# Query projections: the order of the weight halves in two of three token tiles, and the PSUM banks and place of the first two score products

## The chip, the cores and the metric

The kernel runs on one core of a Trainium2 chip. The metric is the time of one execution on the device in microseconds (us). Before the change it is 1845.09 us, the median of three runs (1844.77, 1845.09 and 1849.04).

TensorE (PE in the profile) multiplies, VectorE is DVE, ScalarE is ACT, GpSimd is POOL, and SyncE (SP) issues the transfers. Each engine works through its own instructions in the order of the program and waits on semaphores for the others.

## The reference

A diffusion transformer of two layers for 512 latent and 256 context tokens of width 1024: layer 0 mixes by attention with 16 query and 4 key heads of width 64, layer 1 by a gated recurrence, and each is followed by a gated feed-forward part. The change touches the attention of layer 0 alone. What it computes there is, cut to the core:

```python
def queries(h):
    q = (h @ w_q).reshape(b, t, ATTN_KV_HEADS, ATTN_GROUP, HEAD_DIM).transpose(0, 2, 3, 1, 4)
    return rms_norm(q, q_norm)
...
q_l = apply_axial_rope(queries(h_lat), rope)
k_l, v_l = keys_values(h_lat)
...
s = jnp.einsum('bkgqd,bksd->bkgqs', q, k) * (HEAD_DIM ** -0.5)
p = jax.nn.softmax(s, axis=-1)
return jnp.einsum('bkgqs,bksd->bkgqd', p, v)
```

Queries of context tokens are not rotated, and context tokens attend to context keys alone.

## The kernel before

**Products in three parts.** Every fp32 operand is split into a rounded upper part (`whi`, `hnh`) and the rest (`wlo`, `hnl`), and `mm3` (L110) issues three products for one: upper by upper (L112), upper by lower (L113) and lower by upper (L114). The weights of a group are loaded by `load_split` (L93): a transfer into `raw`, ScalarE rounds it into `whi` (L88), VectorE subtracts for `wlo` (L91). There are three buffers each of `whi` and `wlo`.

**Query projections** (L614 to L636). Four groups (g, 0 to 3) of 256 columns, each with two weight halves: half 0 holds the rows k = 0 to 3 of 8, half 1 the rows 4 to 7. In a group there are three tiles (tp, 0 to 2) of 256 tokens, and each tile is one PSUM bank that holds two runs of 128 tokens (tt). A run is 8 k by 3 products, so 24 matmuls of 256 columns, and a tile is 48. The first run takes half 0 and then half 1; the second run takes half 1 and then half 0. Below, "the tile (2,0)" is group 2, tile 0.

**What follows a tile.** `q_first` (L581) calls `qk_norm_rope` (L502), which is a chain over three engines: ACT squares the product (L510), DVE sums (L513) and scales (L514), ACT takes the root (L515), DVE inverts and refines (L516 to L520) and multiplies the product by it (L522, tile `qhat`, the last reader of the bank), DVE multiplies by the cosines (L532) while POOL multiplies by the sines in four pieces (L537), DVE adds both (L541) and rounds (L585), and POOL subtracts (L586). For context tiles (tp 2) one multiplication on POOL (L526) stands in place of L532 to L541. In the very last tile (3,2), L526 and L586 are on DVE. The transposes of a tile (L592, `ptq`, two banks with four transposes each) and their copies on ACT (L595, into `qT`) come three tiles later (`Q_LAG`, L610). The code is in that order; the framework's scheduler then fixes the order of every engine's instructions, and buffers are given out when one is free.

**The passage to the attention** (L648 to L657). The PSUM pool of the projections (four banks for products, three for transposes, one for another sum, `pa`) is closed, and one of two pairs of banks for scores, two banks and two more is opened on the same eight banks. Three tiles are then still to be transposed ((3,0), (3,1), (3,2)); between the first and the second of them the scores of head 0, tile 0 are issued (`score_mm`, L637, four matmuls, tile `sc`). After it, 96 units (16 heads by 6 tiles of 128 tokens) run through `scores` (maximum on DVE L689, exponential on ACT L691), transposes of the probabilities (L703) and products with the values (L714, L715). Beside them TensorE transposes the residual input in eight blocks (`rx`, L671, copied to `hT` by ACT L672) and sums a modulation product (`pa`, L181); `rx` uses the same two pairs of banks as the scores.

Of the kernel before, what the change touches and what calls it, by code (L numbers as in the profile page):

```python
# [18 lines left out]
KT = D // P  # L19
# [28 lines left out]
def kernel(  # L48
# [13 lines left out]
    def pool(name, es=None, **kw):  # L62
        return (es or ctx).enter_context(tc.tile_pool(name=name, bufs=1, reuse_waits="tile", **kw))
# [5 lines left out]
    def psum_pool(**bufs):  # L69
        es = ExitStack()  # L70
        psums["pool"], psums["bufs"] = pool(f"psum{len(bufs)}", es, space=PSUM), bufs
        return es
# [7 lines left out]
    def bank(name):  # L80
        return psums["pool"].tile([P, 512], F32, tag="b", bufs=psums["bufs"]["b"], name=name)
# [28 lines left out]
    def mm3(ps, ahi, alo, bhi, blo, first, last, onto=False):  # L110
        kw = dict(skip_group_check=True) if onto else {}
        PE.matmul(ps, ahi, bhi, start=first, stop=False, **kw)  # L112
        PE.matmul(ps, ahi, blo, start=False, stop=False, **kw)  # L113
        PE.matmul(ps, alo, bhi, start=False, stop=last, **kw)  # L114
# [436 lines left out]
    def k_first(tp):  # L551
        r = qk_norm_rope(kraw[tp].rearrange("p t (h d) -> p t h d", d=HD), tp, "k")
        kd = qst.tile([P, 2, KVH, 2, HD], F32R, tag="sp", bufs=3, name="kd")
        kl = qst.tile([P, 2, KVH, HD], F32R, tag="spl", name="kl")
        for i in range(2):
            DVE.tensor_copy(kd[:, :, :, i].rearrange("p t h d -> p (t h) d"), r.rearrange("p t h d -> p (t h) d"))
        POOL.tensor_tensor(kl, r, kd[:, :, :, 0].bitcast(F32), op=ALU.subtract)

        def second():
            kds = [kd[:, :, g].rearrange("p t a d -> p t (a d)") for g in range(KVH)]  # L560
            kds += [kl[:, :, 2 * i : 2 * i + 2].rearrange("p t a d -> p t (a d)") for i in range(KVH // 2)]
            cs = slice(tp * 256, tp * 256 + 256)
            for i in range(0, len(kds), 2):
                pt = bank("ptk")
                for j in range(2):
                    for tt in range(2):
                        PE.transpose(pt[:, (2 * j + tt) * P : (2 * j + tt + 1) * P],
                                     kds[i + j][:, tt].bitcast(F32), ident)
                pg = pt.rearrange("p (g t) -> p g t", g=2)
                if i < KVH:  # L570
                    ACT.copy(kTt[:, i : i + 2, cs], pg)
                    continue
                for j in range(2):
                    dst = kTt[:, KVH + j : 2 * KVH : 2, cs]
                    rows = slice(j * HD, (j + 1) * HD)
                    ACT.copy(dst[0:HD], pg[rows])
                    DVE.tensor_copy(dst[HD:P], pg[rows])

        return second
# [18 lines left out]

    pes.close()
    pes = psum_pool(q=4, b=3, a=1)  # L600
    apsum = psums["pool"].tile([P, 512], F32, tag="a", name="pa")

    def qbank(name):
        return psums["pool"].tile([P, 512], F32, tag="q", bufs=psums["bufs"]["q"], name=name)
# [3 lines left out]
    later = []  # L608
# [7 lines left out]
    for g in range(KVH):  # L616
        ws = []
        for i in range(2):
            src = attn_w_qkv[0, 512 * i : 512 * (i + 1), g * 256 : (g + 1) * 256].rearrange("(k p) n -> p k n", p=P)
            ws.append(load_split(src, [P, 4, 256], f"wq{g}{i}"))  # L620
        for tp in range(3):
            psf = qbank(f"q{g}{tp}")
            for tt in range(2):
                ts_ = slice((tp * 2 + tt) * P, (tp * 2 + tt + 1) * P)
                ks = list(range(KT)) if tt == 0 else list(range(4, KT)) + list(range(4))
                for k in ks:
                    wh, wl = ws[k // 4]
                    mm3(psf[:, tt * 256 : tt * 256 + 256], hn_hi[k][:, ts_], hn_lo[k][:, ts_],
                        wh[:, k % 4], wl[:, k % 4], k == ks[0], k == ks[-1])
            if g == 0:  # L630
                first(k_first, tp)
            first(q_first, g, tp, psf[:, 0:512])
            dfill.step(2)
# [3 lines left out]
    def score_mm(h, t):  # L637
        g, j = h // 4, h % 4
        keys = key_tiles(t)
        nk, k0 = len(keys) * P, keys[0] * P  # L640
        q = qT[g][:, j, t * P : (t + 1) * P]
        ps = s2("sc")
        for a in range(0, nk, 512):
            e = min(nk, a + 512)
            PE.matmul(ps[:, a:e], q, kTh[g][:, k0 + a : k0 + e], start=True, stop=False)  # L645
            PE.matmul(ps[:, a:e], q, kTl[g][:, k0 + a : k0 + e], start=False, stop=True)  # L646
        return ps
# [1 line left out]
    dfill.drain()  # L649
    pes.close()  # L650
    pes = psum_pool(s2=2, b=2, t=2)
    early = {}
    for i, f in enumerate(later):
        f()
        if i == 0:
            early[0, i] = score_mm(0, i)
    qes.close()  # L657

    hpool = pool("hT", side="right")
# [1105 lines left out]
```

## Time and profile before

| what | value |
|---|---|
| median of three runs | 1845.09 us |
| the profiled execution, its time | 1847.34 us |
| the profiled execution, its span from first to last instruction | 1845.5 us |
| PE busy | 1780.8 us (96%) |
| DVE busy | 1224.5 us (66%) |
| ACT busy | 765.9 us (42%) |
| POOL busy | 543.2 us (29%) |
| query projections on PE, start to last product | 76.9 to 173.9 us |

The span is counted from the first instruction of the execution. A row of the timeline names the start, the duration, the engine, the line, the operation, output<-input and the shape; in brackets is the idle time of the engine before it and who ended it. The ends of matmuls are modelled, so the pace of TensorE is read from the starts.

### The profile page before, as it was taken

To read this page: it belongs to the slowest core of one execution; us is meant where nothing else is said; L and a number is where in the kernel's file an instruction comes from. 1 tells how busy PE (TensorE), PEld (TensorE's weight loads), DVE (VectorE), ACT (ScalarE), POOL (GpSimd) and SP (SyncE) were. 2 spreads that over 40 slices of the span, in tenths; PEclk is the share of its full clock that TensorE was granted. 3 is DMA by queue.
4 is the path that set the end of the run, shared out by engine and by line. 5 is a ranking of instruction groups with operands and counts; after the bars stand their busy time and mean duration, and the time that the engine had idled before them with its cause. 6 is when DMAs were issued, how large, how long until landed. Compare 5 with 4: busy or idle time off the path is not lost.

```text
span 1845.5 us, 30295 instructions
## 1 busy us (share of the span) xinstructions
PE 1780.8 (96%) x11929; PEld 1627.0 (88%) x11929; DVE 1224.5 (66%) x2097; ACT 765.9 (42%) x1465; POOL 543.2 (29%) x508
## 2 busy tenths in 40 slices
PE   8979999999999999999999989999998999999998
PEld 6779688988899989898988889898997899898997
DVE  3586688888878787878756475656738774344443
ACT  4333787777533425252545233333323432222234
POOL 1244255445513314141315264443535100000000
PEclk9999999999999999999999999999999999999999
DMA  9433510002033232525231212112211253333321
GB/s 329 160 115 86 166 59 24 14 11 75 23 111 112 71 119 75 154 87 171 63 109 45 69 58 81 59 57 80 80 52 29 86 166 92 93 89 94 100 85 56
DMA packets 213198, 166.41 MB, mean 90 GB/s; under 512 B 7696, under 2 KB 190144, under 8 KB 213056
## 3 DMA queue, kind: packets, MB, share of 16 engines
q1 hardware_dynamic: 212768, 163.43, 28.7%
q8 instruction: 94, 1.54, 0.3%
q10 hardware_dynamic: 288, 1.05, 0.1%
q14 instruction: 48, 0.39, 0.1%
HBM read 162.36 MB, written 2.10 MB: 89 GB/s over the span
## 4 chain that ended last, share of the span: by engine, by line
PE 83%; DVE 8%; ACT 3%; POOL 3%; issue 2%; DMA 1%; POOLq 0%; SPq 0%; DVEq 0%; ACTq 0%
PE ffo L112 5%; PE ffo L113 5%; PE ffo L114 5%; PE ffi L112 5%; PE ffi L113 5%; PE ffi L114 5%; PE pt L703 3%; PE x L112 2%; PE x L113 2%; PE x L114 2%; PE lv L1566 2%; PE hz L112 2%; PE hz L113 2%; PE hz L114 2%; PE sc L645 2%
## 5 line engine op out<-in xcount | busy, mean ns | idle before, releaser
L112 PE MATMUL ffi<-fnh,whi_fi 128*128 128x256 f32 x704 | 198.9, 283 | 0.1
L113 PE MATMUL ffi<-fnl,whi_fi 128*128 128x256 f32 x704 | 198.0, 281 | 0.9 <-DVE fnl L1236 0.9
L114 PE MATMUL ffi<-fnh,wlo_fi 128*128 128x256 f32 x704 | 197.8, 281 | 0.0
L113 PEld LDWEIGHTS ffi<-fnl,whi_fi 128*128 128x128 f32 x704 | 133.2, 189 | 1.5 <-DVE fnl L1236 1.3
L112 PEld LDWEIGHTS ffi<-fnh,whi_fi 128*128 128x128 f32 x704 | 132.7, 189 | 0.5 <-issue 0.3
L114 PEld LDWEIGHTS ffi<-fnh,wlo_fi 128*128 128x128 f32 x704 | 132.8, 189 | 0.0
L676 DVE SCALAR_TENSOR_TENSOR hT<-ffo,modc,hT 128x512 f32<-128x512 f32 (+1 forms) x106 | 67.0, 636 | 90.8 <-PE ffo L114 90.7
L1573 POOL TENSOR_TENSOR KD<-KD,tot 128x384 f32<-128x384 f32 x96 | 101.5, 1081 | 67.8 <-ACT kc L1556 66.2
L280 POOL TENSOR_TENSOR rc<-rc,mhalf 128x2 f32<-128x2 f32 (+2 forms) x7 | 6.3, 906 | 379.3 <-DVE rc L278 379.3
L693 POOL TENSOR_SCALAR pf<-pf,st 128x768 f32<-128x768 f32 (+1 forms) x96 | 73.6, 769 | 127.9 <-DVE st L692 91.6
L88 ACT CAST whi_fi<-raw_fi 128x1024 fp32r<-128x1024 f32 x44 | 46.2, 1051 | 146.7 <-PE ffi L113 72.7
L114 PE MATMUL ffo<-gh,wlo_w 128*128 128x512 f32 (+1 forms) x304 | 102.6, 338 | 0.0
L113 PE MATMUL ffo<-gl,whi_w 128*128 128x512 f32 (+1 forms) x304 | 102.3, 337 | 0.0
L112 PE MATMUL ffo<-gh,whi_w 128*128 128x512 f32 (+1 forms) x304 | 101.6, 337 | 0.0
L91 DVE TENSOR_TENSOR ptl<-pt,pth 128x384 fp32r<-128x384 f32 (+1 forms) x160 | 79.8, 523 | 12.4 <-ACT pth L88 11.2
L1556 ACT COPY kc<-KD 128x256 f32<-128x256 f32 x112 | 43.0, 414 | 102.7 <-PE lv L1566 37.6
L689 DVE TENSOR_REDUCE st<-sc 128x1 f32<-128x768 f32 (+1 forms) x96 | 74.2, 773 | 15.3 <-PE sc L646 12.5
L88 ACT CAST pth<-pt 128x384 fp32r<-128x384 f32 (+1 forms) x160 | 69.9, 461 | 34.2 <-PE pt L703 22.4
L235 DVE SCALAR_TENSOR_TENSOR adacc<-adw,csil,adacc 128x512 f32<-128x512 f32 x98 | 82.0, 850 | 2.1 <-DMA adw<-in_ada_w_dram 1.8
L1573 DVE TENSOR_TENSOR QD<-QD,tot 128x256 f32<-128x256 f32 x96 | 55.5, 619 | 41.1 <-PE lv L1566 40.4
L691 ACT ACTIVATE pf<-sc,st 128x768 f32<-128x768 f32 (+1 forms) x96 | 73.4, 765 | 19.3 <-DVE st L689 18.4
L703 PE MATMUL pt<-ident,pf 128*128 128x128 f32 x448 | 72.2, 276 | 5.1 <-DVE ptl L91 3.9
(852 smaller groups left out, 5980.6 us busy)
## 6 DMA issues: line engine op xcount, KB each, us to landing
raw_fi<-in_ffn_w_in_dram SPq DMA_DIRECT2D x44, 512.0 KB, 3.7
adw<-in_ada_w_dram SPq DMA_DIRECT2D x40, 512.0 KB, 4.5
adw<-in_ada_w_dram SPq DMA_DIRECT2D x80, 256.0 KB, 3.1
raw_hz<-in_hgrn_w_in_dram SPq DMA_DIRECT2D x14, 512.0 KB, 3.6
raw_fo<-in_ffn_w_out_dram SPq DMA_DIRECT2D x16, 448.0 KB, 3.8
adr<-in_ada_w_dram SPq DMA_DIRECT2D x16, 256.0 KB, 4.7
adr<-in_ada_w_dram SPq DMA_DIRECT2D x8, 512.0 KB, 6.8
raw_wq<-in_attn_w_qkv_dram SPq DMA_DIRECT2D x8, 512.0 KB, 6.2
```

The costliest lines, as they stand in the source:

```text
L88: ACT.copy(hi, src)
L91: (eng or DVE).tensor_tensor(lo, src, hi.bitcast(F32), op=ALU.subtract)
L112: PE.matmul(ps, ahi, bhi, start=first, stop=False, **kw)
L113: PE.matmul(ps, ahi, blo, start=False, stop=False, **kw)
L114: PE.matmul(ps, alo, bhi, start=False, stop=last, **kw)
L235: pin(DVE.scalar_tensor_tensor(a, raw, cc, a, op0=ALU.mult, op1=ALU.add))
L676: DVE.scalar_tensor_tensor(hT[o][:, a:e], ps, mcol(layer, ch, o, v), hT[o][:, a:e], op0=ALU.mult, op1=ALU.add)
L689: DVE.tensor_reduce(st3[:, 0:1], ps[:, :nk], op=ALU.max, axis=AX.X, negate=True)
L691: ACT.activation(pf, ps[:, :nk], AF.Exp, bias=st3[:, 0:1], accum_out=st3[:, 1:2])
L693: POOL.tensor_scalar(pf, pf, st3[:, 2:3], 1.0, op0=ALU.mult, op1=ALU.mult)
L703: PE.transpose(pt[:, i * P : (i + 1) * P], pf[:, (i0 + i) * P : (i0 + i + 1) * P], ident)
L1573: eng.tensor_tensor(view, view, f, op=ALU.mult)
```

## The change

Three edits. In the tiles 0 and 2 of each group the four half runs are issued as (run 0, half 0), (run 1, half 0), (run 0, half 1), (run 1, half 1); tile 1 keeps the order of before. Since both runs are then open at once in one bank, the second run's first matmul doesn't carry the start flag. One bank of the transposes is allocated ahead of `pa` and of the products, which turns the banks round. And the scores of the tiles 0 and 1 of head 0 are issued ahead of the transposes of the last three tiles.

```diff
--- before.py
+++ after.py
@@ -561,7 +561,7 @@
             kds += [kl[:, :, 2 * i : 2 * i + 2].rearrange("p t a d -> p t (a d)") for i in range(KVH // 2)]
             cs = slice(tp * 256, tp * 256 + 256)
             for i in range(0, len(kds), 2):
-                pt = bank("ptk")
+                pt = ptk0.pop() if ptk0 else bank("ptk")
                 for j in range(2):
                     for tt in range(2):
                         PE.transpose(pt[:, (2 * j + tt) * P : (2 * j + tt + 1) * P],
@@ -598,6 +598,7 @@
 
     pes.close()
     pes = psum_pool(q=4, b=3, a=1)
+    ptk0 = [bank("ptk")]
     apsum = psums["pool"].tile([P, 512], F32, tag="a", name="pa")
 
     def qbank(name):
@@ -620,13 +621,20 @@
             ws.append(load_split(src, [P, 4, 256], f"wq{g}{i}"))
         for tp in range(3):
             psf = qbank(f"q{g}{tp}")
-            for tt in range(2):
+            half = [range(4), range(4, KT)]
+            if tp == 1:
+                runs = [(0, half[0]), (0, half[1]), (1, half[1]), (1, half[0])]
+            else:
+                runs = [(0, half[0]), (1, half[0]), (0, half[1]), (1, half[1])]
+            seen = [0, 0]
+            for tt, ks in runs:
                 ts_ = slice((tp * 2 + tt) * P, (tp * 2 + tt + 1) * P)
-                ks = list(range(KT)) if tt == 0 else list(range(4, KT)) + list(range(4))
                 for k in ks:
                     wh, wl = ws[k // 4]
+                    seen[tt] += 1
+                    onto = tp != 1 and tt == 1
                     mm3(psf[:, tt * 256 : tt * 256 + 256], hn_hi[k][:, ts_], hn_lo[k][:, ts_],
-                        wh[:, k % 4], wl[:, k % 4], k == ks[0], k == ks[-1])
+                        wh[:, k % 4], wl[:, k % 4], seen[tt] == 1 and not onto, seen[tt] == KT, tp != 1)
             if g == 0:
                 first(k_first, tp)
             first(q_first, g, tp, psf[:, 0:512])
@@ -649,11 +657,9 @@
     dfill.drain()
     pes.close()
     pes = psum_pool(s2=2, b=2, t=2)
-    early = {}
-    for i, f in enumerate(later):
+    early = {(0, t): score_mm(0, t) for t in range(2)}
+    for f in later:
         f()
-        if i == 0:
-            early[0, i] = score_mm(0, i)
     qes.close()
 
     hpool = pool("hT", side="right")
```

On TensorE, in the tile (2,0) from its tenth to its fifteenth matmul, the rows of before are these (`q_1440` is the tile's bank, `whi_wq_1429` and `wlo_wq_1430` are weight half 0 of group 2, `whi_wq_1435` and `wlo_wq_1436` half 1):

```order
L112 MATMUL q_1440<-whi_wq_1429,hnh_90 128x256
L113 MATMUL q_1440<-wlo_wq_1430,hnh_90 128x256
L114 MATMUL q_1440<-whi_wq_1429,hnl_98 128x256
L112 MATMUL q_1440<-whi_wq_1435,hnh_91 128x256
L113 MATMUL q_1440<-wlo_wq_1436,hnh_91 128x256
L114 MATMUL q_1440<-whi_wq_1435,hnl_99 128x256
```

And after it, from the 22nd to the 27th matmul of the same tile:

```order
L112 MATMUL q_1440<-whi_wq_1429,hnh_90 128x256
L113 MATMUL q_1440<-wlo_wq_1430,hnh_90 128x256
L114 MATMUL q_1440<-whi_wq_1429,hnl_98 128x256
L112 MATMUL q_1440<-whi_wq_1435,hnh_91 128x256
L113 MATMUL q_1440<-wlo_wq_1436,hnh_91 128x256
L114 MATMUL q_1440<-whi_wq_1435,hnl_99 128x256
```

The first use of half 1 moved from the 13th to the 25th matmul of the tile. Half 1 of a group takes the buffers of a half of the group before that is last read at the 36th matmul of that group's last tile before, and at the 24th after.

On VectorE one instruction moves, the subtraction for half 1 of group 2. The names are those of the chain of the tile (1,1), whose L532, L541 and L585 these are; L513 and L514 belong to the tile (1,2):

```order
 L532 TENSOR_TENSOR qrot<-qhat,cwq 128x256 x2
+L91 TENSOR_TENSOR wlo_wq_1436<-raw_wq_1434,whi_wq_1435 128x1024
 L541 TENSOR_TENSOR qrot<-qrot,qsin 128x512
 L585 CAST qd<-qrot 128x8x64
-L91 TENSOR_TENSOR wlo_wq_1436<-raw_wq_1434,whi_wq_1435 128x1024
 L513 TENSOR_REDUCE ss<-qrot 128x8
 L514 TENSOR_SCALAR ss<-ss 128x8
```

It stands ahead of the addition now, and behind the rounding before. All other subtractions for query weights keep their places.

On TensorE, behind the last product of the projections, the rows of before are these (`ptq` are transposes of query tiles, `sc` scores, `rx` blocks of the residual input):

```order
L592 MATMUL ptq<-ident,qd 128x128 x16
L645 MATMUL sc<-kT,qT_705 128x512
L646 MATMUL sc<-kT,qT_705 128x512
L645 MATMUL sc<-kT,qT_705 128x256
L646 MATMUL sc<-kT,qT_705 128x256
L592 MATMUL ptq<-ident,qd 128x128 x8
L671 MATMUL rx_2040<-ident,hT_2004 128x128 x2
L592 MATMUL ptq<-ident,qd 128x128 x8
L671 MATMUL rx_2040<-ident,hT_2004 128x128 x4
L181 MATMUL pa<-adw_2120,cpad 32x256 x4
```

And after, where all lines behind the inserted ones have moved by up to eight numbers (L653 is L645 of before):

```order
L592 MATMUL ptq<-ident,qd 128x128 x8
L653 MATMUL sc<-kT,qT_705 128x512
L654 MATMUL sc<-kT,qT_705 128x512
L653 MATMUL sc<-kT,qT_705 128x256
L654 MATMUL sc<-kT,qT_705 128x256
L653 MATMUL sc<-kT,qT_705 128x512
L654 MATMUL sc<-kT,qT_705 128x512
L653 MATMUL sc<-kT,qT_705 128x256
L654 MATMUL sc<-kT,qT_705 128x256
L592 MATMUL ptq<-ident,qd 128x128 x24
L181 MATMUL pa<-adw_2120,cpad 32x256 x4
```

Two scores stand ahead of the 24 transposes of group 3, and no `rx` block stands among them. In the built program the scores' pairs are the banks 0 to 3, which held transposes and `pa` before the passage; the transposes of group 3 alternate between the banks 4 and 5, and bank 5 held the product of the tile (3,2). Before the change, the first scores' pair held the products of (3,1) and (3,2), and the transposes' banks held `pa` and the product of (2,2).

On ScalarE the copy of the first `rx` block stood ahead of the load of the exponential's table and of the first two exponentials; it stands behind them now, so three copies of `rx` blocks stand between the second and the third exponential, and two stood there before. The first `rx` block now takes the bank pair of the first scores and waits for their exponential; the second waits for the second's. From about the 960th of some 10,100 rows of TensorE on, the order of all engines is that of before; that place is at 222 us of the profile.

## Rows read from the trace of the kernel before

**Rows 1.** The page's part on the chain that ended last, shares of the span by engine.

```profile
PE 83%; DVE 8%; ACT 3%; POOL 3%; issue 2%; DMA 1%; POOLq 0%; SPq 0%; DVEq 0%; ACTq 0%
```

**Rows 2.** Who TensorE waited for, longest first: engine, line, releaser, us in total, times, longest. The first two rows are from 60 to 200 us, the third is the only row of the stretch from 182 to 222 us.

```profile
PE q L113 <- DVE wlo_wq L91: 5.1, 1, 5.1
PE sc L645 <- DVE qhat L522: 3.5, 1, 3.5
...
PE pt L703 <- DVE ptl L91: 1.3, 2, 1.1
```

**Rows 3.** The timeline of TensorE in the tile (2,0), and the first matmul of the tile (3,0).

```profile
128.63 0.28 PE L113 MATMUL q<-wlo_wq,hnh 128*128 128x256 f32 x1
...
129.81 0.28 PE L114 MATMUL q<-whi_wq,hnl 128*128 128x256 f32 x1
129.92 0.31 PE L112 MATMUL q<-whi_wq,hnh 128*128 128x256 f32 x1
135.38 0.58 PE L113 MATMUL q<-wlo_wq,hnh 128*128 128x256 f32 x1 [5.15 <-DVE wlo_wq L91]
...
141.05 1.04 PE L592 MATMUL ptq<-ident,qd 128*128 128x128 f32 x8
...
154.81 0.36 PE L112 MATMUL q<-whi_wq,hnh 128*128 128x256 f32 x1
```

**Rows 4.** Stretches: length, busy time of PE, its weight loads, DVE, ACT and POOL (instructions), TensorE's granted clock, DMA share, GB/s.

```profile
135.30:138.50 3.20, 3.12 (x14) 3.12 (x15) 3.03 (x9) 0.21 (x1) 1.18 (x1) 0.50 0.51 165
...
179.20:182.40 3.20, 3.20 (x15) 3.05 (x16) 2.68 (x4) 0.80 (x2) 0.00 (x0) 0.57 1.20 302
```

**Rows 5.** ACT's rounding and DVE's subtraction of weight halves: half 1 of group 2 on ACT, then half 1 of group 3 on ACT and on DVE.

```profile
128.74 1.05 ACT L88 CAST whi_wq<-raw_wq 128x1024 fp32r<-128x1024 f32 x1
...
152.82 1.05 ACT L88 CAST whi_wq<-raw_wq 128x1024 fp32r<-128x1024 f32 x1 [2.83 <-PE q L114]
...
155.31 1.22 DVE L91 TENSOR_TENSOR wlo_wq<-raw_wq,whi_wq 128x1024 fp32r<-128x1024 f32 x1
```

**Rows 6.** The timeline of DVE over the end of the chain of the tile (1,1), all of (1,2) and the start of (2,0). The first L91 is half 1 of group 2, the second half 0 of group 3.

```profile
130.82 1.02 DVE L532 TENSOR_TENSOR qrot<-qhat,cwq 128x256 f32<-128x256 f32 x2
133.03 0.69 DVE L541 TENSOR_TENSOR qrot<-qrot,qsin 128x512 f32<-128x512 f32 x1 [1.19 <-POOL qsin L537]
...
134.10 1.22 DVE L91 TENSOR_TENSOR wlo_wq<-raw_wq,whi_wq 128x1024 fp32r<-128x1024 f32 x1
135.24 0.68 DVE L513 TENSOR_REDUCE ss<-qrot 128x8 f32<-128x512 f32 x1
...
136.42 1.21 DVE L91 TENSOR_TENSOR wlo_wq<-raw_wq,whi_wq 128x1024 fp32r<-128x1024 f32 x1
...
140.83 0.43 DVE L585 CAST qd<-qrot 128x512 fp32r<-128x512 f32 x1 [1.48 <-POOL qrot L526]
141.94 0.69 DVE L513 TENSOR_REDUCE ss<-qrot 128x8 f32<-128x512 f32 x1 [0.69 <-ACT qrot L510]
```

**Rows 7.** The timelines of POOL and DVE: two instructions of POOL beside those of rows 6, and an earlier pair, a subtraction on DVE beside a multiplication on POOL, and POOL's subtraction where DVE does no L91.

```profile
130.86 2.14 POOL L537 TENSOR_TENSOR qsin<-qhat,swq 128x128 f32<-128x128 f32 x4 [3.46 <-DVE qhat L522]
134.33 2.14 POOL L586 TENSOR_TENSOR qd<-qrot,qd 128x512 fp32r<-128x512 f32 x1 [1.33 <-DVE qd L585]
141.34 1.30 POOL L586 TENSOR_TENSOR qd<-qrot,qd 128x512 fp32r<-128x512 f32 x1 [0.54 <-DVE qd L585]
...
110.98 1.28 POOL L526 TENSOR_TENSOR qrot<-qhat,wk 128x512 f32<-128x512 f32 x1 [2.22 <-DVE qhat L522]
111.45 1.90 DVE L91 TENSOR_TENSOR wlo_wq<-raw_wq,whi_wq 128x1024 fp32r<-128x1024 f32 x1 [0.61 <-ACT whi_wq L88]
```

**Rows 8.** Who DVE waited for from 142 to 181.5 us, all rows, columns as in rows 2.

```profile
DVE qrot L541 <- POOL qsin L537: 4.0, 4, 1.2
DVE ss L516 <- ACT ss L515: 1.6, 6, 0.3
DVE qd L585 <- POOL qrot L526: 1.5, 1, 1.5
DVE ss L513 <- ACT qrot L510: 0.7, 1, 0.7
```

**Rows 9.** The last instruction of the last tile's chain, on DVE.

```profile
180.48 0.69 DVE L586 TENSOR_TENSOR qd<-qrot,qd 128x512 fp32r<-128x512 f32 x1
```

**Rows 10.** TensorE from the last product of the projections on.

```profile
173.74 1.91 PE L592 MATMUL ptq<-ident,qd 128*128 128x128 f32 x16
...
179.17 0.50 PE L645 MATMUL sc<-kT,qT 128*128 128x512 f32 x1 [3.52 <-DVE qhat L522]
...
180.24 1.91 PE L592 MATMUL ptq<-ident,qd 128*128 128x128 f32 x8
```

**Rows 11.** ScalarE in the passage: copies of query transposes, of an `rx` block, the table load, the first and the third exponential.

```profile
183.35 1.07 ACT L595 CAST qT<-ptq 128x512 fp32r<-128x512 f32 x2 [0.57 <-PE ptq L592]
184.31 0.82 ACT L672 COPY hT<-rx 128x768 f32<-128x768 f32 x1
185.14 1.28 ACT L691 ACT_TABLE_LOAD   x1
186.44 0.90 ACT L691 ACTIVATE pf<-sc,st 128x768 f32<-128x768 f32 x1
...
190.87 0.91 ACT L691 ACTIVATE pf<-sc,st 128x768 f32<-128x768 f32 x1
```

## The prediction

> **What bounds the kernel now.** The chain that ended last comes first: TensorE carries 83% of it [rows 1], so an edit is worth what it takes from TensorE's own time or from its waits. So I read who TensorE waited for in the stretch that the change touches. Two waits stand out, 5.1 us on the lower part of a weight half and 3.5 us on the last read of the last query product [rows 2]; the edits aim at one each. The timeline shows the first in the tile (2,0): thirteen matmuls, then nothing from 129.92 until 135.38 us [rows 3]. It costs more than its 5.15 us: the fourteen matmuls behind it run at a granted clock of 0.50, the lower of the two levels (1.2 GHz), and take 3.1 us [rows 4]. At the pace ahead of the wait, ten matmuls from 128.63 to 129.81 [rows 3], so 0.118 us each, they would take 1.65 us. The clock adds about 1.5 us.
>
> Then comes the question who sets the pace from there to the end of the projections, and here the reader should look at VectorE. From 142 to 181.5 us it waits 7.8 us in all: 4.0 and 1.5 us for POOL and 1.6 us for ScalarE's root inside its own chain, and 0.7 us, once, for a square that had to wait for TensorE's product [rows 8]. So TensorE holds the chain of the query tiles up once. All that an earlier TensorE can hand it is 0.7 us.
>
> **First term: the tile (2,0).** Now 24 matmuls need half 0 alone. TensorE stands at 129.92 with twelve of them done, so it reaches half 1 at 129.92 + 11 x 0.118 = 131.3 us. ScalarE has rounded half 1 by 128.74 + 1.05 = 129.8 [rows 5]; its place in ScalarE's order is the same and the earlier release of the buffer doesn't help, since ScalarE was busy with other things until then. The subtraction now stands behind L532, which ends at 130.82 + 1.02 = 131.84 [rows 6], and not at 134.10. It takes 1.22 us there, but POOL's four multiplications run from 130.86 to 133.00 [rows 7]. An earlier pair shows what this does: a subtraction that began at 111.45 beside a POOL instruction ending at 110.98 + 1.28 = 112.26 took 1.90 us; and POOL's L586 took 2.14 us beside a subtraction, and 1.30 alone [rows 7]. So the two don't run together. With a piece of POOL of some 0.45 us in front, I take the subtraction as done at 133.3 (133.06 if nothing is in its way, 133.74 if it takes 1.90). TensorE waits 2.0 us instead of 5.15 us, and the tile ends at 133.35 + 24 x 0.118 = 136.2 instead of 141.05 [rows 3]: 4.9 us earlier, 3.4 us if the clock falls all the same.
>
> **Second term: VectorE's chain, where that lead ends.** POOL's last two pieces run after the subtraction: 133.3 + 0.9 = 134.2. So L541, which waits for them, starts 1.1 us later than 133.03 [rows 6]. L585 follows, and L513 of the next tile no longer has a subtraction of 1.22 us ahead of it: it starts at 135.25 instead of 135.24, no change. POOL's L586 begins later but alone, so it ends at 136.75 instead of 134.33 + 2.14 = 136.47, and the next subtraction, at 136.42 before, starts 0.3 us late. L585 of (1,2) comes at 141.1 instead of 140.83, and L513 of the tile (2,0) at once, at 141.45 instead of 141.94, since its product has been there for 5 us. But now its L514 meets L586 on POOL, which was over before, and that gives the 0.5 us back. From then on the chain is that of before, 0.1 us late. Bounds: if POOL and the subtraction don't disturb each other, L513 of (1,2) comes 1.05 us early and the chain stays so; if the 1.1 us of L541 is never caught up, it is 1.1 us late. I take 0.1 us late, by the rows of the nearest pairs.
>
> The Trainium skill (SBUF — State Buffer, section "Who interferes with whom") says that a VectorE instruction with two inputs in SBUF and a POOL instruction that reads SBUF exclude each other, and that whoever is issued first holds the port for the whole instruction. The rows above agree for L91 against L526 and L586. By the rule the moved subtraction pushes L541 back by 1.1 us; without it the sum would be about 1.1 us lower.
>
> **Third term: group 3.** TensorE now comes 4.9 us early to the tile (3,0), at 149.9 instead of 154.81 [rows 3], and is through half 0 at 149.9 + 24 x 0.118 = 152.7. ScalarE may round half 1 earlier than 152.82, where it waited 2.83 us for TensorE; but the subtraction keeps its place on VectorE behind the chain of (2,1), at 155.31 + 1.22 = 156.5 [rows 5], plus the 0.1. So TensorE waits 3.9 us there: the wait of 5.15 us is taken out of group 2 and put into group 3. Such a pause costs clock again (up to 1.5 us). The tile ends between 159.4 and 160.9, where 154.81 + 48 x 0.118 + 0.3 of a short stall made 160.8. Of 4.9 us between nothing and 1.4 us reach the last tile, and even these only lengthen the wait for VectorE below.
>
> **Fourth term: the passage.** The chain of (3,2) on VectorE ends at 180.48 + 0.69 = 181.17 [rows 9], plus 0.1. The first scores now need only two transpose banks copied by ScalarE, so both, and the first four transposes of (3,0), are done by about 176.5 (173.74 and eight transposes, the copies and these three). The next four go to bank 5, which held the product of (3,2), and wait for its last read at 179.12: the wait of 3.52 us [rows 10] stays, about 3 us long and further on in the order. Done under it are the scores twice, 0.7 us each (six times 256 columns at 0.118 us), and four transposes, 0.5 us (sixteen take 1.91 us [rows 10]). After it come five blocks of four transposes at the lowered clock (0.57 from 179.2 on [rows 4]; eight take 1.91 us there [rows 10]), each waiting for the copy of the block two ahead. By 0.9 us a block, some 0.2 us to hand over (an estimate) and 0.55 us a copy (half of 1.07) the last copy ends near 184.0; before, at 183.35 + 1.07 = 184.4 [rows 11]. The table load follows at once instead of behind the first `rx` copy (184.31, 0.82 us), so the first exponential starts at 185.3 instead of 186.44, 1.1 us early. That is partly given back: the first `rx` block must wait for that exponential (186.3), and three copies of 0.8 us and two hand-overs to TensorE stand between the second and the third exponential. With about 0.95 us for an exponential, 3 x 0.8 for copies and 0.9 for the waits the third starts at 190.6 instead of 190.87 [rows 11]: 0.3 us early; TensorE's next scores about 0.5 us. I take 0.4 us. Bounds: 1.1 us gained, as the first exponential, or 0.8 us lost, if ScalarE gets no earlier and the third copy counts in full. Up to 222 us TensorE waited only 1.3 us in the attention [rows 2], so it has little else to win, and behind that the order is the same and carries any shift to the end.
>
> **Sum.** 0.1 us lost and 0.4 us gained: 0.3 us faster. The profiled execution took 1847.34 us with a span of 1845.5, so 1847.0 is what it becomes; the median of the runs shown lies 2.25 us below it, and the same difference from 1845.09 gives 1844.8 us. About 0.3% (5.5 us) is what a measurement of this kernel can tell from no change, so this counts as none.
>
> **Rivals.**
> *Both stalls go, as the two waits suggest.* 4.9 us in group 2 and 3.5 us in the passage: 8.4 us, 1836.7 us. For it: TensorE has 83% of the chain. Against it: rows 8; the subtraction of group 3 and the last read stand at the end of VectorE's chain. Chance 0.09.
> *VectorE and POOL don't disturb each other, and the early table load is kept.* 1.05 + 1.1 = 2.2 us, 1842.9 us. For it: 1.05 us is the distance that the subtraction no longer stands in front of L513. Against it: the 1.90 and 2.14 us of rows 7. Chance 0.15.
> *Slower: the moved subtraction.* It cuts in between POOL's second and third piece at 131.84; its 1.1 us on L541 goes through the serial chain to 181.17, if L585 and L513 don't catch it up, and the three copies in a row cost 0.8 us: 1.9 us, 1847.0 us. It decides from the point where L513 of (2,0) starts later than 141.94. Against it: the 1.22 us that no longer stand between L585 and L513. Chance 0.16.
>
> **How the numbers follow.** The forecast has 0.60, within 1.5 us of 1844.8. The range is 1840.5 to 1848.0: it takes in the second and the third rival with 1 to 2.4 us about them for the runs and for the new order up to 222 us, and leaves out the first. Faster by over 0.3% is the first rival and little else, 0.10; slower by over 0.3% has no case with a price, 0.04; no change 0.86.
>
> **What will show it.** In the changed profile: the wait in the tile (2,0) falls to about 2 us, after 24 matmuls; a new one of 3 to 4 us stands in (3,0) after 24 matmuls, on a subtraction; L541 of (1,1) starts near 134.2; L513 of (2,0) follows L585 without a wait and within 0.5 us of 141.5; TensorE still waits for L522 of (3,2), near 179, in the middle of the transposes; the first exponential is about 1 us early, the third 0 to 1. If (3,0) shows no wait, or L522 of (3,2) ends well ahead of 178, VectorE's chain isn't the bound and the forecast is wrong; if the third exponential is later than 191.5, the slower rival is right.

## The result and the profile after

The changed kernel takes 1849.51 us (median of 22 runs, 1847.10 to 1853.48), the kernel before beside it 1847.11 us (22 runs); the ratio is 1.0014, with an interval of 1.0009 to 1.0020. So the change costs about 2.4 us. The forecast was 1844.8, and the range ended at 1848.0: the time lies outside. The forecast stood on a median of three runs, 1845.09 us; the 22 runs here put the kernel before 2.0 us higher. The profiled execution took 1853.48 us with a span of 1851.7; 1.85 us of that is a later start, as the marks below show.

The chain by engine first, which answers to [rows 1]:

```profile
PE 81%; DVE 9%; ACT 4%; POOL 3%; issue 2%; DMA 1%; SPq 0%; POOLq 0%; DVEq 0%; ACTq 0%
```

It says little: TensorE has lost two points to VectorE and ScalarE. The next view is who TensorE waited for, 60 to 200 us, columns as in [rows 2]:

```profile
PE q L112 <- DVE vv L91: 3.6, 1, 3.6
PE q L113 <- DVE wlo_wq L91: 3.5, 1, 3.5
PE pta L189 <- ACT kT L571: 3.2, 1, 3.2
PE ptq L592 <- DVE qhat L522: 1.8, 1, 1.8
...
```

The wait for half 1 is 3.5 us instead of 5.1 (and in group 3 instead of group 2), the one for the last `qhat` 1.8 instead of 3.5. But a new one heads the list: the first query product waits 3.6 us for `vv`, VectorE's subtraction of the v values. Nothing in the prediction names it. The timelines of both kernels show the place. L463 is a small copy ahead of the change, here the mark from which times are counted, since the two executions reach it 1.85 us apart. Before:

```profile
76.57 0.18 DVE L463 COPY cols<-pr 128x32 f32<-128x32 f32 x1
76.90 0.36 PE L112 MATMUL q<-whi_wq,hnh 128*128 128x256 f32 x1 [0.61 <-DVE cols L463]
79.14 0.68 DVE L91 TENSOR_TENSOR vv<-kv,vv 128x512 fp32r<-128x512 f32 x1
82.73 0.42 PE L181 MATMUL pa<-adw,cpad 128*32 128x256 f32 x4
82.89 0.60 ACT L510 ACTIVATE qrot<-q 128x512 f32<-128x512 f32 x1 [2.95 <-PE q L114]
83.51 1.28 ACT L515 ACT_TABLE_LOAD   x1
85.00 0.68 DVE L513 TENSOR_REDUCE ss<-qrot 128x8 f32<-128x512 f32 x1
```

and after:

```profile
78.42 0.18 DVE L463 COPY cols<-pr 128x32 f32<-128x32 f32 x1
80.99 0.68 DVE L91 TENSOR_TENSOR vv<-kv,vv 128x512 fp32r<-128x512 f32 x1
81.72 0.58 PE L112 MATMUL q<-whi_wq,hnh 128*128 128x256 f32 x1 [3.58 <-DVE vv L91]
90.35 0.42 PE L181 MATMUL pa<-adw,cpad 128*32 128x256 f32 x4
90.51 0.60 ACT L510 ACTIVATE qrot<-q 128x512 f32<-128x512 f32 x1 [8.72 <-PE q L114]
91.12 1.28 ACT L515 ACT_TABLE_LOAD   x1
91.14 0.69 DVE L513 TENSOR_REDUCE ss<-qrot 128x8 f32<-128x512 f32 x1 [4.20 <-ACT qrot L510]
```

The third `vv` has kept its place behind the mark (2.57 us). It reads the last pair of `kv` banks, in the built program 4 and 5. The bank held for the first keys' transposes takes bank 0, the query banks turn to 4 to 7, and the first of them, bank 4, is the one that this subtraction still reads. Before, the first product went to bank 1, free since the mark. The Trainium skill (PSUM — Partial Sum Buffer, section "Summary: rules for kernel authors") wants a different bank where PSUM is read while a matmul runs. The 3.58 us are what one bank for both costs here.

The second half of the loss is in the clock. Stretches of before and after, columns as in [rows 4]:

```profile
76.90:82.60 5.70, 5.70 (x48) 5.69 (x48) 4.81 (x16) 3.00 (x6) 2.13 (x4) 1.00 0.00 1
```

```profile
81.70:87.90 6.20, 6.17 (x29) 6.18 (x30) 4.67 (x13) 0.09 (x1) 3.05 (x4) 0.50 0.00 0
```

Before, 48 matmuls take 5.7 us at a granted clock of 1.00; after, 29 take 6.2 us at 0.50, the lower level (1.2 GHz). The sum at the entry, counted from the mark: the product starts 2.97 us later (81.72 - 78.42 against 76.90 - 76.57), and its tile takes 2.8 us longer (8.63 to the `pa` behind it, against 5.83). Before, L513 had 1.5 us to spare behind ScalarE's square (85.00 - 83.49); that is used up. What is left, 4.3 us, is the shift of L513: 91.14 - 78.42 against 85.00 - 76.57. Some 0.35 us more come at ScalarE's root: the load of its table (second last rows), which follows the square, was over 1.1 us before VectorE had the sum ready and now ends 0.4 us after it.

From there on VectorE's chain carries the shift through all twelve tiles nearly unchanged: `qhat` is 4.64 us late in the tile (0,0), 4.66 in (1,1), 4.63 in (2,0) and 4.64 in (3,2). Around the moved subtraction the chain looks like this, to be held against [rows 6] and [rows 7]:

```profile
137.38 3.13 POOL L537 TENSOR_TENSOR qsin<-qhat,swq 128x128 f32<-128x128 f32 x4 [3.45 <-DVE qhat L522]
...
138.28 1.48 DVE L91 TENSOR_TENSOR wlo_wq<-raw_wq,whi_wq 128x1024 fp32r<-128x1024 f32 x1
140.54 0.69 DVE L541 TENSOR_TENSOR qrot<-qrot,qsin 128x512 f32<-128x512 f32 x1 [0.77 <-POOL qsin L537]
...
141.60 0.68 DVE L513 TENSOR_REDUCE ss<-qrot 128x8 f32<-128x512 f32 x1
...
184.92 0.69 DVE L522 TENSOR_TENSOR qhat<-q,ss 128x512 f32<-128x512 f32 x1
```

L541 is 5.66 us late, a good 1.0 more than `qhat` ahead of it, and L513 of the next tile is back at 4.5: the moved subtraction costs its 1.0 us and gives it back, as forecast. The Trainium skill (SBUF — State Buffer, section "Who interferes with whom") says that a VectorE instruction with two inputs in SBUF contends with a GpSimd instruction that reads SBUF. POOL's 3.13 us, where [rows 7] have 2.14, agree.

Last, TensorE and ScalarE in group 3 and in the passage, against [rows 10] and [rows 11]; the first row is the last `qhat` of before, to set beside the 184.92 above:

```profile
178.43 0.69 DVE L522 TENSOR_TENSOR qhat<-q,ss 128x512 f32<-128x512 f32 x1
```

```profile
163.04 0.58 PE L113 MATMUL q<-wlo_wq,hnh 128*128 128x256 f32 x1 [3.50 <-DVE wlo_wq L91]
...
185.67 0.33 PE L592 MATMUL ptq<-ident,qd 128*128 128x128 f32 x1 [1.83 <-DVE qhat L522]
...
189.95 0.59 ACT L595 CAST qT<-ptq 128x512 fp32r<-128x512 f32 x1 [0.35 <-PE ptq L592]
190.55 1.28 ACT L697 ACT_TABLE_LOAD   x1
191.85 0.90 ACT L697 ACTIVATE pf<-sc,st 128x768 f32<-128x768 f32 x1
...
197.15 0.91 ACT L697 ACTIVATE pf<-sc,st 128x768 f32<-128x768 f32 x1
```

From the last `qhat` it is 6.93 us to the first exponential and 12.23 to the third, where it was 8.01 and 12.44. So the passage gains 1.1 and 0.2 us.

### The profile page after: what moved, and what is told of

Read it like the earlier page. It is cut to its first block, busy times and chain, and to the rows that moved or that the text cites. A ratio compares the mean times of both kernels' runs of the same rounds, so it can differ in the third digit from the quotient of the medians.

```text
span 1851.7 us, 30295 instructions
## 1 busy us (share of the span) xinstructions
PE 1783.8 (96%) x11929; PEld 1630.8 (88%) x11929; DVE 1225.4 (66%) x2097; ACT 765.3 (41%) x1465; POOL 542.9 (29%) x508
## 4 chain that ended last, share of the span: by engine, by line
PE 81%; DVE 9%; ACT 4%; POOL 3%; issue 2%; DMA 1%; SPq 0%; POOLq 0%; DVEq 0%; ACTq 0%
PE ffo L112 5%; PE ffo L113 5%; PE ffo L114 5%; PE ffi L112 5%; PE ffi L113 5%; PE ffi L114 4%; PE pt L709 3%; PE x L112 2%; PE x L113 2%; PE x L114 2%; PE lv L1572 2%; PE hz L112 2%; PE hz L113 2%; PE hz L114 2%; PE y L114 1%
## 5 line engine op out<-in xcount | busy, mean ns | idle before, releaser
L91 DVE TENSOR_TENSOR ptl<-pt,pth 128x384 fp32r<-128x384 f32 (+1 forms) x160 | 79.7, 523 | 12.4 <-ACT pth L88 11.3
```

The lines of the kernel that those rows point to most:

```text
L91: (eng or DVE).tensor_tensor(lo, src, hi.bitcast(F32), op=ALU.subtract)
```

## The experiments

This table is worked out from the traces of all runs: us from the mark L463 to the first query `qhat`, to that of (3,2), to the first exponential and to the last of the attention. A second figure is a second execution of the same kernel (three for after). Then the median. The medians come from four sittings, each beside the kernel before: the first of after (before at 1847.11); the first product in bank 0 (first figure), halves, banks and scores, and ScalarE copies (1847.32); the second figures of after and of bank 0, GpSimd copies (first figure) and half 0 (1847.75); the rest (1846.95). The later single executions of before, after, banks and scores, and the split without halves took 1847.66, 1850.21, 1849.00 and 1847.11 us.

| run | qhat (0,0) | qhat (3,2) | first exp | last exp | median, us |
|---|---|---|---|---|---|
| before | 10.71; 10.71 | 101.86; 101.93 | 109.87; 109.94 | 344.85; 344.98 | 1847.11 |
| after | 15.35; 14.00; 15.16 | 106.50; 105.05; 106.16 | 113.43; 111.97; 113.08 | 348.93; 347.77; 348.71 | 1849.51; 1849.70 |
| first product in bank 0 | 10.71; 10.72 | 101.69; 101.85 | 108.07; 107.79 | 343.74; 343.60 | 1844.98; 1846.61 |
| halves alone | 10.72 | 101.73 | 110.82 | 345.99 | 1846.90 |
| banks and scores alone | 14.08; 14.88 | 105.01; 106.07 | 111.86; 112.97 | 347.46; 348.47 | 1849.20 |
| ScalarE copies | 10.71 | 103.96 | 111.35 | 346.80 | 1848.62 |
| POOL copies third tiles | 10.74; 10.71 | 99.44; 100.37 | 105.39; 106.31 | 341.16; 341.91 | 1846.79; 1845.44 |
| the same, without halves | 10.70 | 101.27 | 107.21 | 343.34 | 1847.12 |
| and POOL subtracts half 0 | 10.72 | 102.11 | 108.05 | 343.73 | 1847.30 |
| and VectorE a quarter of L537 | 10.70 | 97.04 | 103.80 | 339.32 | 1841.83 |
| the same, without halves | 10.70; 10.73 | 98.08; 99.76 | 104.02; 105.70 | 339.54; 341.60 | 1842.76 |

**The entry: the first product in another bank.** The held bank goes to q(0,0), not to the keys:

```diff
-                pt = ptk0.pop() if ptk0 else bank("ptk")
+                pt = bank("ptk")
...
-            psf = qbank(f"q{g}{tp}")
+            psf = ptk0.pop() if ptk0 else qbank(f"q{g}{tp}")
```

> The kernel after with one thing changed: the first query product q(0,0) is written into the bank that was held for the first keys' transposes (bank 0, long read), not into bank 4, which VectorE's third v subtraction still reads. All else of the change stays. Theory (the loss sits at the entry: 3.58 us of wait on that subtraction, then 29 matmuls at the low clock, which VectorE's chain carries to the first score): both stretches go, the first qhat of the queries comes 4.2 to 4.3 us earlier against the v subtraction, and the time is 1844.5 to 1846.5 us, 0.9975 to 0.9997 of the kernel before, with the first exponential as in the prediction. Rival 1 (the loss is the subtraction L91 of half 1 that went ahead of L541 and slowed GpSimd): nothing changes, 1849.5. Rival 2 (the shift was the start of that one execution): 1849.5 too, and the trace shows the first scores as late as in the kernel after.

> The run with the first product in bank 0 once more, beside the changed kernel on one chip. Theory: 1844.5 to 1846 us, 0.9980 to 0.9995 of the kernel before and 3 to 5 us under the changed kernel; no wait at q(0,0). Rival (the first result was luck of some runs): 1847 to 1849.

1844.98 us, 0.9991 of before (0.9983 to 1.0000), and beside the changed kernel (1849.70) 1846.61, 0.9995 (0.9987 to 1.0004). In the first profile TensorE's waits from 60 to 200 us have no `vv` any more; the product follows the transpose at L462 at once (under the name of the held tile, `ptk`):

```profile
76.99 0.24 PE L462 MATMUL pr<-ident,rows 32*128 32x32 f32 x1
77.17 0.39 PE L112 MATMUL ptk<-whi_wq,hnh 128*128 128x256 f32 x1
...
179.21 0.69 DVE L522 TENSOR_TENSOR qhat<-q,ss 128x512 f32<-128x512 f32 x1
```

One bank number gives back 4.5 us (1849.51 to 1844.98) and, in the second comparison, 3.1 (1849.70 to 1846.61). From 0.5 to 1.0 us of it arise at the exit: the later query banks turn too, and from the last `qhat` to the first exponential it is 6.38 and 5.94 us instead of 6.93. Both rivals fall: the moved subtraction is still in place, the second execution starts even later than the first profile of after (mark at 78.55 against 78.42), and `qhat` of (3,2) is on time in both. The second median is a little above the 1846 expected.

**The halves alone.** The kernel before with only the new order of the `runs`.

> The first part of the change alone on the kernel before: the first and last token tiles by weight halves, with the weight buffers and the place of half 1's subtraction that follow from it; banks and scores as before. Theory (VectorE's chain sets the first score, the weight wait of tile (2,0) is hidden under it): the 5.1 us wait for half 1 in tile (2,0) shrinks below 1 us, qhat(3,2) stays within 0.5 us of the kernel before, 1846.6 to 1848.0 us. Rival (the waits of TensorE are on the path): 4 to 5 us faster, 1842 to 1843. Second rival (the moved subtraction costs its 1.0 us to the end): 1848.0 to 1848.5 with qhat(3,2) 1 us late.

1846.90 us, 0.9999 (0.9990 to 1.0008): nothing. Its waits and a stretch of the passage:

```profile
PE q L113 <- DVE wlo_wq L91: 5.2, 2, 3.5
...
PE sc L652 <- DVE qhat L522: 3.2, 1, 3.2
```

```profile
182.00:186.00 4.00, 4.00 (x20) 4.00 (x19) 1.37 (x2) 1.76 (x3) 0.00 (x0) 0.50 0.60 146
```

The 5.1 us of [rows 2] have become 1.7 in (2,0) and 3.5 in (3,0): split, not saved, and the 1.7 is more than the 1 us expected. `qhat` of (3,2) is 0.13 us early, so neither a gain nor a lasting loss comes out of the moved subtraction. The first exponential is 0.95 us late all the same; there the granted clock is 0.50 for the whole stretch, and 0.69 in the like stretch of before (180.54 to 184.54).

**Banks and scores alone.** The other two edits on the kernel before.

> The second and third parts alone on the kernel before: one bank of the transposes is taken first, so that the query banks turn, and two scores are issued early; the token tiles run over the halves as before. Theory (the turn of the banks costs at the entry): the wait of q(0,0) for the third v subtraction is there with 3 to 4 us and the low clock behind it, and the time is that of the kernel after within 1 us, 1848.5 to 1850.5. Rival (the halves cost): 0.4 us faster than the kernel before, 1846.7, since only the passage's gain is left.

> Banks and scores alone on the kernel before, for a second execution. Theory (chance): the clock falls near 498 us with a chance of some 0.6. Rival (it belongs to the halves with the turned banks): it stays at 1.00. The entry's wait of 3.6 us again.

1849.20 us, 1.0010 (1.0001 to 1.0019), the time of the changed kernel; the wait is there in both executions (3.59 us in each):

```profile
80.02 0.44 PE L112 MATMUL q<-whi_wq,hnh 128*128 128x256 f32 x1 [3.59 <-DVE vv L91]
```

So the loss belongs to the turn of the banks, and the halves have no part in it; nor have the two early scores, which the run with the first product in bank 0 has too, without the loss.

**The changed kernel again.**

> The changed kernel once more, unedited, for a second profiled execution. Theory (entry): the wait of q(0,0) for the third v subtraction is there again with 3.4 to 3.8 us, and the stretch at the low clock behind it, whose length changes from execution to execution (28 matmuls at 0.21 us in the first profile, some 16 in the run with the banks alone), so the first qhat of the queries lies 13 to 15.4 us behind the copy of the columns at L463 (10.7 in the kernel before) and the time is 1848.5 to 1850 us, 2 to 4.5 us above the run with the first product in bank 0. Rival (the first profile was one disturbed execution): no wait at q(0,0), and the time 1847.

> The changed kernel, unedited, for a third profiled execution. Theory (chance): the clock behind the 2.1 us wait near 498 us may stay at 1.00. Rival (it belongs to the change): it falls again, 1.5 us. The entry as before: a wait of 3.5 to 3.7 us at q(0,0) and 14 to 15.4 us from the copy at L463 to the first qhat of the queries.

The wait of 3.58 to 3.59 us is there each time. What differs is the low clock behind it: 16 matmuls and 3.4 us here, 29 and 6.2 us in the first profile:

```profile
80.10:83.50 3.40, 3.31 (x16) 3.31 (x16) 2.97 (x9) 0.15 (x1) 2.13 (x5) 0.52 0.00 0
```

Hence a loss of 3.2 to 4.6 us at (3,2) from one cause.

**Is VectorE's chain the bound? Three ways to shorten it,** all with the first product in bank 0. First, ScalarE makes the copy L585: `ACT.copy(qd[:, :, :, g % 2], r)`.

> As the run with the first product in bank 0, and besides ScalarE, not VectorE, makes the first copy of the rotated queries (L585, 11 times 0.43 us, and 4.4 us in which VectorE waits at it for GpSimd's L526). Theory (VectorE's chain is what bounds the stretch between the first query product and the first score): the chain is 4 to 9 us shorter, until TensorE's own work ends it; the first score comes 2 to 5 us earlier than in that run and the time is 1840 to 1843.5 us. Rival (TensorE is the bound there): the same time as that run within 0.5 us. Rival (ScalarE's squares now queue behind the copies): 1 to 2 us slower than that run.

1848.62 us, 3.6 us more than without it: the last rival, at twice its price. The copy stands in ScalarE's queue ahead of the next tile's square. The waits of ScalarE and then of VectorE, 84 to 180 us:

```profile
ACT qd L585 <- DVE qrot L541: 30.4, 7, 5.7
...
ACT qd L585 <- POOL qrot L526: 8.5, 3, 3.3
```

```profile
DVE ss L513 <- ACT qrot L510: 10.2, 7, 2.6
```

VectorE has lost 4.7 us of work (11 copies of 0.43) and the 4.4 us of waits at L585, and got 10.2 us of waits that were not there; `qhat` of (3,2) is 2.1 to 2.3 us later. The chain runs through queues, and work taken off an engine may come back as a wait.

Second, GpSimd, which makes the rotation and the remainder of the third tiles anyway, makes the copy between them: `(eng if tp == 2 else DVE).tensor_copy(qd[:, :, :, g % 2], r)`.

> As the run with the first product in bank 0, and besides GpSimd, which makes the rotation L526 of every group's third tile and its remainder L586, makes the copy between them (L585) too, so that VectorE no longer waits there 1.5 us and copies 0.43 us, in groups 0 to 2. Theory (VectorE's chain is the bound from the first query product to the first score): the half 1 subtraction of group 3 comes 2 x 1.9 = 3.8 us earlier, TensorE with it, and qhat(3,2) 3 to 5 us earlier against L463 (101.7 us behind it in the run this is built on); the time is 1840.5 to 1843 us. Rival (TensorE is as much the bound): less than 1 us, 1844.5 to 1846. Rival (GpSimd's third operation slows VectorE beside it and comes late itself): 1846 or more.

> The run in which GpSimd copies the third tiles once more, beside three like it on one chip. Theory: qhat(3,2) again 99.4 us behind the copy at L463 (101.86 in the kernel before), the last exponential of the attention 3.5 to 3.9 us earlier against L463 than in the kernel before, and the time 1843.5 to 1846 us, 0.998 to 0.9992 of the kernel before. Rival (the gain is given back later): the exponentials as early, and 1846.5 to 1848.

1846.79 and 1845.44 us, 0.9991 (0.9981 to 1.0000) and 0.9990 (0.9981 to 0.9999). VectorE's waits from 84 to 180 us, without the copy on GpSimd and with it:

```profile
DVE qrot L541 <- POOL qsin L537: 8.2, 9, 1.6
DVE qd L585 <- POOL qrot L526: 4.4, 3, 1.5
...
```

```profile
DVE qrot L541 <- POOL qsin L537: 8.6, 9, 1.6
...
```

The 4.4 us at L585 are gone, and the chain up to the first score is shorter, so it was the bound there; but `qhat` of (3,2) gains 1.3 to 2.4 us, not 3 to 5. The time doesn't show the gain: 1846.79 misses the 1840.5 to 1843 us expected and lies beside 1846.61 for bank 0 alone in the same sitting. The second, 1845.44, is in its own range, but its `qhat` and its last exponential (2.9 to 3.1 us early, 3.5 to 3.9 expected) fall short. A third tile saves about 0.8 us, not 1.9: from its `qhat` to the next it is 4.5 to 4.6 us where it was 5.3 to 5.4. (One in the second execution saves nothing, 5.62 us: there VectorE waits 2.0 us for the square of a late product.) The timelines in the tile behind the first of them show why, first without the copy on GpSimd, then with it:

```profile
120.59 0.74 DVE L514 TENSOR_SCALAR ss<-ss 128x8 f32<-128x8 f32 x1
...
122.24 0.17 DVE L519 TENSOR_SCALAR ss<-ss 128x8 f32<-128x8 f32 x1
```

```profile
118.04 0.82 DVE L514 TENSOR_SCALAR ss<-ss 128x8 f32<-128x8 f32 x1
119.60 1.28 POOL L586 TENSOR_TENSOR qd<-qrot,qd 128x512 fp32r<-128x512 f32 x1
119.78 1.12 DVE L519 TENSOR_SCALAR ss<-ss 128x8 f32<-128x8 f32 x1
```

L514 was long already, beside L586. What is new is L519: it now falls beside L586, ends with it (120.90 and 120.88), and takes 1.12 us instead of 0.17.

Third, on top of that, once GpSimd subtracts half 0 of the weights, and once VectorE makes one of the four products at L537 (`DVE if tt == 1 and b == 1 and nm == "q" else POOL`).

> As the run in which GpSimd copies the third tiles, and besides GpSimd, not VectorE, subtracts half 0 of the query weights of groups 1 to 3 (L91, 1.2 to 1.5 us on VectorE each). Theory (VectorE's chain): another 2 to 4 us, 1837 to 1841. Rival (GpSimd's queue: its subtraction of 1024 columns, some 2.6 us by twice its 512 column row, sits ahead of L537, for which VectorE waits): 1 to 4 us slower than the run it is built on.

> As the run in which GpSimd copies the third tiles, and besides VectorE makes one of the four products at L537 in the first two tiles of each group, whose end VectorE waits for 0.8 to 1.6 us at L541 (8.6 us in nine waits). Theory (VectorE's chain with its waits for GpSimd is still the bound): each wait shrinks by 0.5 us, less the 0.3 us of the product, 0.2 to 0.5 us a tile, 1 to 3 us in all: qhat(3,2) 96.5 to 98.5 us behind L463. Rival (TensorE ends the stretch now): less than 0.5 us. Rival (the product on VectorE costs as much as the wait): 0 to 1 us later.

The first is the rival: GpSimd needs 2.38 us for each subtraction, and `qhat` of (3,2) comes 1.7 to 2.7 us later than without it; the time, 1847.30 beside 1846.79, hardly changes. The second is the best version of all: 1841.83 us, 0.9972 (0.9961 to 0.9984), some 7.7 us under the changed kernel and 3.6 under the version without the split product, timed beside it. VectorE's waits, 84 to 180 us:

```profile
...
DVE ss L516 <- ACT ss L515: 2.5, 9, 0.3
DVE qrot L541 <- POOL qsin L537: 1.9, 5, 0.5
...
```

8.6 us of waits at L541 have become 1.9.

**What are the halves worth then?** Both shortened versions without them:

> As that run (first product in bank 0, GpSimd copies the third tiles, banks turned, two scores early), but without the weight halves: all token tiles in the order of the kernel before. Theory (the halves are worth something only where VectorE's chain no longer hides TensorE's wait): TensorE waits 4 to 5 us for half 1 in tile (2,0), its products come late to a chain that is 3.8 us shorter, and qhat(3,2) lies 0.5 to 2 us later than with the halves, 100 to 101.5 us behind L463. Rival (the chain still hides the wait): qhat(3,2) at 99.4 within 0.3 us, the same time.

> As the run before it, without the weight halves. Theory (TensorE's wait comes onto the path as the chain gets shorter): 1 to 4 us later at qhat(3,2) than with the halves, 98.5 to 101.5 us behind L463. Rival (the chain still hides it): the same within 0.3 us.

> First product in bank 0, GpSimd's copy of the third tiles and the split product, without the halves, for a second execution. Theory (chance): the clock falls near 490 us with a chance of some 0.6. Rival (it belongs to the halves): it stays at 1.00. qhat(3,2) again 98.1 us behind the copy at L463 within 0.5 us, 1 us later than with the halves.

With GpSimd's copy, `qhat` of (3,2) is 0.9 to 1.8 us later without the halves, with the split product 1.0 and 2.7 us. The second execution of the latter missed its 98.1 us by 1.7: there TensorE waited 3.5 us in one piece for half 1, and 0.8 at most in the other execution. The medians, 1847.12 against 1845.44 and 1842.76 against 1841.83, point the same way, though their intervals overlap. So the halves are worth 1 to 3 us at (3,2) once VectorE is no longer in front, and nothing ahead of that; in the time such a gain isn't shown.

**A second step.** In the first profiles another 1.5 us appeared behind 495 us, in the kernels with halves and turned banks and in no other. TensorE waits 2.1 us there for ScalarE in all of them:

> The kernel before, unedited, for a second profiled execution. Theory (the clock's fall near 495 us is chance of an execution): by nine of fourteen executions so far it falls here too with a chance of some 0.6: the window of 5 us behind the 2.1 us wait shows a granted clock of 0.66 to 0.9. Rival (it belongs to the halves with the turned banks): 1.00, as in the first execution. The query chain as before: qhat(3,2) 101.9 us behind the copy at L463.

The wait in the kernel before, then the 5 us behind it in that kernel, in the second profile of after and in its third:

```profile
495.28 0.44 PE L112 MATMUL x<-xt2h,whi_w 128*128 128x384 f32 x1 [2.11 <-ACT c L941]
```

```profile
495.30:500.30 5.00, 5.00 (x29) 5.00 (x30) 5.00 (x10) 2.76 (x6) 1.02 (x1) 1.00 0.07 19
```

```profile
498.40:503.40 5.00, 4.96 (x19) 4.96 (x20) 5.00 (x10) 2.83 (x6) 0.95 (x1) 0.66 0.08 22
```

```profile
499.30:504.30 5.00, 4.97 (x29) 4.97 (x30) 5.00 (x10) 2.82 (x6) 0.96 (x1) 1.00 0.07 14
```

One kernel, one wait, two clocks. Of the four further executions three stayed at 1.00 (before, after, banks and scores); in the fourth, the split version without halves, the clock fell (0.66), though in that kernel's first execution it hadn't. So the step is no fixed cost of the change. That the change has no part in it isn't shown: the fall came in nine of ten profiles of kernels with both halves and turned banks, and in one of the eight others.

## Why the prediction was wrong

- **The sum** ("0.1 us lost and 0.4 us gained") lacks a term, and that is the error. The prediction weighs where the new banks lie only in its fourth term, at the exit, where transposes go to bank 5. At the entry the same turn puts the first product on a bank that is still read: it starts 2.97 us later, and the clock adds 1.4 to 2.8 us and the table load 0.35, less 1.5 us of slack: 3.2 to 4.6 us. The prediction asked what an earlier TensorE could hand to VectorE's chain (0.7 us), and not whether TensorE could come later. The trace of before was enough for it: the third `vv` ends at 79.14 + 0.68 = 79.82, 2.9 us behind the start of the first product at 76.90. What it left out was to ask of each of the twelve products who reads its bank last; of the first that is another stage.
- **The base.** Forecast and measurement differ by 4.7 us. Of these 2.0 are the median of three runs (1845.09, against 1847.11 beside the changed kernel), and 2.7 are the change: 0.3 us faster was forecast, 2.4 slower came.
- **"From then on the chain is that of before"** is right in its place: the halves alone and the first product in bank 0 put `qhat` of (3,2) 0.0 to 0.2 us early, where 0.1 late was forecast. That the chain carries a delay unchanged is also why the missed term came through in full: a chain that hides TensorE's gains hides none of its own losses.
- **First term.** 2.0 us of wait in (2,0) were forecast; with the first product on time it is 1.7 (5.2 in two waits, the longer 3.5). In after itself it is not seen, since TensorE came 6 us late. (129.92 + 11 x 0.118 makes 131.2, not 131.3; nothing hangs on it.)
- **Third term.** 3.9 us in (3,0) forecast, 3.5 measured, and 2.8 in the second profile.
- **Fourth term.** The first exponential 1.1 us early and the third 0.3: measured, from the last `qhat`, 1.1 and 0.2. The wait for L522 amid the transposes stays, 1.8 us in the first and third profiles and 3.3 in the second, where about 3 was forecast. With the first product in bank 0 the last product lies in bank 6, so the transposes don't wait for it (they wait 1.6 to 1.8 us for `qd`, L586), and from the last `qhat` the first exponential gains 1.6 to 2.1 us.
- **The rivals.** The slower one (1.9 us) came near the size by luck: the moved subtraction loses its 1.0 us and gives it back. Its sign, a third exponential later than 191.5, came true (197.15, or 195.30 without the later start) and pointed to the wrong cause. "Both stalls go" fell with the halves alone. The rival without disturbance fell with POOL's 3.13 us and the subtraction's 1.48.
- **The forecast itself** fits the kernel with the first product in bank 0 better: 0.3 us faster was forecast, and both intervals (0.9983 to 1.0000 and 0.9987 to 1.0004) hold that. Its profiles gain more, 1.1 to 1.4 us at the last exponential.

Left open: from the mark to the last exponential the changed kernel loses 2.8 to 4.1 us in its profiles, while the medians differ by 2.4 and 2.0.

## What to carry to other kernels

When a change takes or frees one PSUM bank, the tiles behind it can all move to other banks, as here: go through the stage's first tiles as well as its last, and ask of each bank who reads it last, in the stage ahead too. A wait of TensorE that stands beside another engine's serial chain is worth nothing until that chain is shorter; shorten it first (here a copy kept on the engine that makes both its neighbours, and a product divided between two engines), then take the wait. And count a new wait of TensorE with the clock behind it, at the lower level's price.

## What was not expected of the hardware

- The clock behind a wait differs from execution to execution. Behind 3.6 us at the entry it fell in each of five profiles, but for 3.4 us in one and 6.2 us in another of the same kernel. Behind 2.1 us near 495 us it fell in 10 of 18 profiles, for 1.5 us each. So two profiles of the same kernel can differ by 1 to 3 us through the clock alone.
- GpSimd holds up VectorE's small instructions too: a `TENSOR_SCALAR` of 128x8 took 0.17 us alone and 1.12 us beside a GpSimd subtraction, with which it ended. So an operation moved to GpSimd saved 0.8 us of the 1.9 that VectorE had spent on it.
